# Low parts of the weights of q, k, v, z and gates: a negated copy by ScalarE and an adding transfer in place of VectorE's subtraction

## The chip, the cores and the metric

One core of a Trainium2 chip runs the whole program. The metric is the device time of one execution in microseconds (us). The engines are TensorE (PE; its weight loads are PEld), VectorE (DVE), ScalarE (ACT), GpSimd (POOL) and SyncE (SP); a q behind a name (SPq, ACTq, POOLq) is the engine's own queue, from which it issues DMAs.

## What is computed

One layer of a hybrid backbone in fp32, with 512 latent and 256 context tokens and a model width of 1024. Cut to what matters here:

```
h  = modulate(rms(x,   norm_attn), mod_x[0], mod_x[1])
hc = modulate(rms(ctx, norm_attn), mod_c[0], mod_c[1])
qkv, z, beta, decay, cq, ckv, k_rope, gates = split(h @ w_in)   # and the same of hc
q, k, v = silu(conv5(qkv)); q, k l2-normed                      # 8 heads of 128
o_gdn   = chunked gated delta rule over q, k, v, forwards and backwards
o_mla   = softmax attention of 8 heads with low-rank q and kv
y = sigmoid(g_gdn) * (gdn_out(o_gdn, z) @ w_bg) + sigmoid(g_mla) * (o_mla @ w_bm)
x = x + mod_x[2] * (y @ w_out)
x = x + mod_x[5] * (relu(modulate(rms(x)) @ w_mlp_in)^2 @ w_mlp_out)
```

## The kernel before

Products with weights are made in three matmuls in a rounded fp32 format (fp32r). Both factors are split into a high part, which is the value rounded to that format, and a low part, which is what the rounding took away. `mm3` (lines 183 to 186) adds high by high, high by low and low by high into one PSUM bank.

`wchunk` (lines 165 to 180) brings weights in chunks of 128x512 fp32, 256 KB. For each chunk there are three steps: SyncE issues the load into `wf` (line 177, four buffers), ScalarE writes the high part `wh` (line 178, three buffers), and VectorE, or for some weights GpSimd, writes the low part `wl` (line 179, three buffers). A buffer of `wh` or `wl` is free again when TensorE's last matmul has read it, a buffer of `wf` when the low part has been made:

```
nc.sync.dma_start(wf.rearrange("p (k n) -> p k n", k=step), src[:, k:k + step])
act.copy(wh, wf)
eng.tensor_tensor(wl, wf, f32(wh), ALU.subtract)
```

`project` multiplies 128 output columns, that is two such chunks, with the 512 latent tokens (matmuls of 512 columns) and, for k and v, with the 256 context tokens as well. `gdn_in` does that for the k, v and q of a pair of heads; `convolve` then takes the result from PSUM (lines 466 and 468, ScalarE), applies the five-tap convolution (line 471, four instructions of VectorE) and the silu (lines 473 and 474), and `transposes` (line 487) turns the result. `gdn_gram` builds the decay and the Gram matrices: GpSimd selects the triangles `rh` (line 566), TensorE multiplies them (line 571), ScalarE takes Exp (line 577) and VectorE multiplies (lines 584 and 590). `gdn_prep` inverts a triangular matrix, in 30 steps of VectorE (lines 629 and 630) and several small products. `gdn_chain` runs the recurrence over six blocks in both directions: GpSimd selects `Em` and `Qm` (line 727), TensorE multiplies (lines 751, 766, 786, 802, 805), VectorE makes `rho` (758), the state (794) and the output `ob` (812, 813), ScalarE `y` (773, 778). `power` (line 149) is a power on GpSimd; one of its results is `nk`.

`z_chunk` and `gate_chunk` project the eight groups of 128 columns of z and the sixteen of the gates and store them in DRAM. They have the lowest priority and fill TensorE's time between the parts of the recurrence. In all 48 such groups, 96 chunks, belong to k, v, q, z and gates.

The order of the work is not the code's: a scheduler puts all instructions into a fixed order on each engine, from the code's dependencies, its priorities and estimates of its own. On the chip each engine keeps that order and waits at an instruction until its inputs are there and its output buffer is free. A change of one instruction can therefore move others on every engine.

Of the kernel before, what the change touches and what calls it, by code (L numbers as in the profile page):

```python
# [9 lines left out]
AF = mybir.ActivationFunctionType  # L10
ALU = mybir.AluOpType
# [4 lines left out]
P = 128  # L16
LOW = 1000000
AHEAD = 100
KT = 8
# [59 lines left out]
def f32(ap):  # L79
    return ap.bitcast(F32)  # L80
# [3 lines left out]
def tile_layer(ctx, tc, I, out, stop=None, dbg=None):  # L84
    nc = tc.nc
    act = nc.scalar
    dve = nc.vector
    pool = nc.gpsimd
# [12 lines left out]
    def bank(tag):  # L101
        return ps.tile([P, 512], F32, tag=tag, name=tag, bufs=banks[tag])

    def v4(t):
        return t.rearrange("p (a b) -> p a b", b=128)
# [41 lines left out]
    def power(out_ap, in_ap, n, half):  # L147
        e = expt[:, 1 if half else 0, 0:n]
        pool.tensor_tensor(out_ap, in_ap, e, ALU.pow)
# [12 lines left out]

    WN = 512

    def wchunk(src, nk=KT, n=P, eng=dve, keep=None):

        step = min(nk, WN // n)
        res = []
        for k in range(0, nk, step):
            wf = wp.tile([P, WN], F32, tag="wf", name="wf", bufs=4)[:, :step * n]  # L170
            if keep is None:
                wh = wp.tile([P, WN], F32R, tag="wh", name="wh", bufs=3)[:, :step * n]
                wl = wp.tile([P, WN], F32R, tag="wl", name="wl", bufs=3)[:, :step * n]
            else:
                wh = keep.tile([P, WN], F32R, tag="kh", name="kh", bufs=2 * KEEP)
                wl = keep.tile([P, WN], F32R, tag="kl", name="kl", bufs=2 * KEEP)
            nc.sync.dma_start(wf.rearrange("p (k n) -> p k n", k=step), src[:, k:k + step])
            act.copy(wh, wf)  # L178
            eng.tensor_tensor(wl, wf, f32(wh), ALU.subtract)  # L179
            res += [(wh[:, n * i:n * i + n], wl[:, n * i:n * i + n]) for i in range(step)]  # L180
        return res

    def mm3(po, lh, ll, rh, rl, first, last):
        pe.matmul(po, lh, rh, start=first, stop=False)  # L184
        pe.matmul(po, lh, rl, start=False, stop=False)  # L185
        pe.matmul(po, ll, rh, start=False, stop=last)  # L186
# [148 lines left out]
    for qf in range(4):  # L335
        kts = (qf, qf + 4)
        modulation(qf)
        if qf == 0:
            for k in range(0, KT, 4):
                nc.sync.dma_start(ct[:, k:k + 4, :], I["cxT"][:, k:k + 4, :])  # L340
        for kt in kts:
            modulate(kt, xt, NL, rx, hTh, hTl, 0)
        w = [wchunk(I["w_nat"][:, kt:kt + 1, 384:736], 1, 352) for kt in kts]
        natural(pos1[:4], kts, w)
        if qf == 0:
            rc = rms(ct, NC, 1, "c")
        for kt in kts:
            modulate(kt, ct, NC, rc, cTh, cTl, 1)
        natural(pos1[4:], kts, w)
        if qf == 1:  # L350
            nc.sync.dma_start(mk[:, ncol:], I["masks"][:, ncol:])
            nc.sync.dma_start(mk2, I["early"])
# [57 lines left out]
    for kt in order:  # L410
        natural(pos0, (kt,), [wchunk(I["w_nat"][:, kt:kt + 1, 0:384], 1, 384)])
# [28 lines left out]
    def project(chunk, with_ctx):  # L440
        pl = bank("d")
        pc = bank("d")[:, :NC] if with_ctx else None
        for k0 in (0, 4):
            for kt in range(k0, k0 + 4):
                mm3(pl, *chunk[kt], hTh[:, kt, :], hTl[:, kt, :], kt == 0, kt == KT - 1)
            if with_ctx:
                for kt in range(k0, k0 + 4):
                    mm3(pc, *chunk[kt], cTh[:, kt, :], cTl[:, kt, :], kt == 0, kt == KT - 1)
        return pl, pc
# [12 lines left out]
    def convolve(pl, pc, ch, dst):  # L462

        o = 0 if pc is not None else NC + GAP
        n = NG - o
        act.copy(raw[:, GAP + NC + GAP:GAP + NG], pl)  # L466
        if pc is not None:
            act.copy(raw[:, GAP:GAP + NC], pc)
        act.activation(dst, raw[:, o + 2:o + 2 + n], AF.Identity, scale=convh[:, ch, 2:3])
        for i in (0, 1, 3, 4):  # L470
            dve.scalar_tensor_tensor(dst, raw[:, o + i:o + i + n], convh[:, ch, i:i + 1], dst, ALU.mult, ALU.add)  # L471
        tt = raw[:, o + 2:o + 2 + n]
        act.activation(tt, dst, AF.Tanh)
        dve.scalar_tensor_tensor(dst, tt, 1.0, dst, ALU.add, ALU.mult)
        if pc is not None:
            pool.memset(raw[:, GAP + NC:GAP + NC + GAP], 0.0)

    def transposes(src, nb, tag):

        res = []  # L480
        b = 0
        while b < nb:
            n = min(4, nb - b)
            t = bank(tag)
            for q in range(n):
                c = at(b + q) if nb == 6 else 128 * (b + q)
                pe.transpose(t[:, 128 * q:128 * q + 128], src[:, c:c + 128], ident)  # L487
            res.append((t, b, n))
            b += n
        return res  # L490

    def gdn_in(pr):
        kT = gp.tile([P, 2, NG], F32, tag="kT", name="kT", bufs=2)
        qT = gp.tile([P, 2, NL], F32, tag="qT", name="qT", bufs=2)
        kn = gp.tile([P, 2, 6, P], F32, tag="kn", name="kn", bufs=2)
        vn = gp.tile([P, 2, 6, P], F32, tag="vn", name="vn", bufs=2)
        ssq = gp.tile([P, 2, 6], F32, tag="ssq", name="ssq", bufs=2)
        ssk = gp.tile([P, 2, 6], F32, tag="ssk", name="ssk", bufs=2)
        nk = gp.tile([P, 2, 6], F32, tag="nk", name="nk", bufs=2)
        r2 = gp.tile([P, 2, 6], F32, tag="r2", name="r2", bufs=2)  # L500
        junk = gx.tile([P, P], F32, tag="junk", name="junk")
        for h in range(2):
            hd = 2 * pr + h
            pl, pc = project(wchunk(I["w_qkv"][8 + hd]), True)
            convolve(pl, pc, 8 + hd, kT[:, h, :])
            for t, b, n in transposes(kT[:, h, :], 6, "t"):
                act.copy(kn[:, h, b:b + n, :], v4(t)[:, :n, :])
                for q in range(n):
                    act.activation(junk, kn[:, h, b + q, :], AF.Square, accum_out=ssk[:, h, b + q:b + q + 1])
            dve.tensor_scalar(ssk[:, h, :], ssk[:, h, :], EPS, None, op0=ALU.add)  # L510
            power(nk[:, h, :], ssk[:, h, :], 6, True)
            dve.reciprocal(r2[:, h, :], ssk[:, h, :])
        res = (kT, qT, kn, vn, ssq, ssk, nk, r2)
        gram = gdn_gram(pr, res)
        for h in range(2):
            hd = 2 * pr + h
            vT = gx.tile([P, NG], F32, tag="vT", name="vT")
            pl, pc = project(wchunk(I["w_qkv"][16 + hd]), True)
            convolve(pl, pc, 16 + hd, vT)
            for t, b, n in transposes(vT, 6, "t"):  # L520
                for q in range(n):
                    act.activation(vn[:, h, b + q, :], t[:, 128 * q:128 * q + 128], AF.Copy,
                                   scale=nk[:, h, b + q:b + q + 1])
        for h in range(2):
            hd = 2 * pr + h
            pl, _ = project(wchunk(I["w_qkv"][hd]), False)
            convolve(pl, None, hd, qT[:, h, :])
            for t, b, n in transposes(qT[:, h, :], 4, "t"):
                for q in range(n):
                    act.activation(junk, t[:, 128 * q:128 * q + 128], AF.Square,  # L530
                                   accum_out=ssq[:, h, b + q:b + q + 1])
        return res, gram
# [311 lines left out]
            act.dma_start(d_y[:, hd, :], tz)  # L844

    def gate_chunk(i):
        pz, _ = project(wchunk(I["w_gate"][i]), False)
        tz = gy.tile([P, NL], F32, tag="tanh", name="tg")
        act.activation(tz, pz, AF.Tanh, scale=0.5)
        nc.sync.dma_start(d_gate[i], tz)  # L850

    def z_chunk(hd):
        pz, _ = project(wchunk(I["w_z"][hd]), False)
        tz = gy.tile([P, NL], F32, tag="tanh", name="tz")
        act.activation(tz, pz, AF.Tanh, scale=0.5)
        dve.scalar_tensor_tensor(tz, tz, 1.0, pz, ALU.add, ALU.mult)
        nc.sync.dma_start(d_z[hd], tz)
# [5 lines left out]
    def fill(pr):  # L863
        for kind, i in fills[pr]:
            if kind == "z":
                z_chunk(i)
            else:
                gate_chunk(i)

    ops0, gram0 = gdn_in(0)  # L870
    prep0 = gdn_prep(0, ops0, gram0)
    ops1, gram1 = gdn_in(1)
    with low():
        fill(0)
    gdn_out(0, gdn_chain(0, ops0, prep0))
    prep1 = gdn_prep(1, ops1, gram1)
    ops2, gram2 = gdn_in(2)
    with low():
        fill(1)
# [495 lines left out]
```

## Time and profile before

| what | value |
|---|---|
| median of three runs | 1333.8 us (1332.42 to 1333.87) |
| profiled execution, its own time | 1332.53 us |
| its span in the profile | 1330.7 us |
| mean granted clock of TensorE | 0.984 |
| TensorE busy | 1269.9 us, 95% of the span |
| VectorE busy | 867.2 us, 65% |
| ScalarE busy | 648.2 us, 49% |
| GpSimd busy | 278.5 us, 21% |
| line 179 on VectorE, all weights | 268 instructions, 182.9 us |
| line 178 on ScalarE, all weights | 292 instructions, 177.1 us |

The span is the time from the first to the last instruction in the trace; the execution's own time is 1.8 us longer. Busy time is the time in which an engine worked on instructions. A TensorE that is busy is not always at its peak, because matmuls overlap and their ends are modelled. The granted clock is the share of TensorE's full clock that the chip allowed. A group gives its line, engine, operation and operands, then its busy time and the mean of one in ns, then the idle time of the engine just before and what ended it.

### The profile page before, as it was taken

How to read it: one execution, taken by the hardware profiler on the slowest of the kernel's cores; microseconds unless marked ns; L12 is line 12 of the kernel's file. 1: busy time of each engine (PE TensorE's matmuls, PEld its weight loads, DVE VectorE, ACT ScalarE, POOL GpSimd, SP SyncE). 2: the span in 40 equal slices, each digit the busy share in tenths (PEclk: the TensorE clock that was granted, in tenths of full speed). 3: DMA queues.
4: the chain of work that ended last, by engine and by line, in shares of the span. 5: the costliest groups of instructions: out<-in, count | busy, mean ns of one | idle time of the engine just before them, and what ended most of it. 6: DMA issues, size and time to landing. Idle time of an engine off the chain costs nothing.

```text
span 1330.7 us, 21029 instructions
## 1 busy us (share of the span) xinstructions
PE 1269.9 (95%) x7430; PEld 1112.8 (84%) x7430; DVE 867.2 (65%) x1861; ACT 648.2 (49%) x1666; POOL 278.5 (21%) x372
## 2 busy tenths in 40 slices
PE   5899899998999999989999999999999999999998
PEld 4798787887888888879899998888997888888886
DVE  4656798866688678747778788676885333333332
ACT  4557575336653675356667576323443242242331
POOL 0022423223410431113112221222041010010110
PEclk9999998988999999999999999999999999999999
DMA  9333225210233124441011013766452222222232
GB/s 359 112 110 88 56 71 128 94 41 9 88 103 104 49 76 120 123 143 60 14 46 37 9 40 131 266 209 249 173 177 95 95 95 95 95 96 95 96 112 86
DMA packets 97993, 141.20 MB, mean 106 GB/s; under 512 B 32736, under 2 KB 41952, under 8 KB 97760
## 3 DMA queue, kind: packets, MB, share of 16 engines
q1 hardware_dynamic: 68576, 127.27, 28.8%
q10 hardware_dynamic: 29312, 12.59, 3.8%
q8 instruction: 59, 0.97, 0.3%
q14 instruction: 46, 0.38, 0.1%
HBM read 124.23 MB, written 15.60 MB: 105 GB/s over the span
## 4 chain that ended last, share of the span: by engine, by line
PE 82%; DVE 7%; DMA 4%; ACT 4%; issue 1%; POOL 1%; SPq 0%; DVEq 0%; ACTq 0%; POOLq 0%
PE d L184 20%; PE d L185 20%; PE d L186 20%; DMA wm<-in_w_mod 2%; PE p L184 1%; PE c L766 1%; PE p L185 1%; PE p L186 1%; PE c L786 1%; PE p L1046 1%; PE c L751 1%; PE e L802 1%; DVE kT L471 1%; PE e L805 1%; PE t L487 1%
## 5 line engine op out<-in xcount | busy, mean ns | idle before, releaser
L178 ACT CAST wh<-wf 128x512 fp32r<-128x512 f32 (+2 forms) x292 | 177.1, 610 | 352.2 <-PE d L185 307.4
L179 DVE TENSOR_TENSOR wl<-wf,wh 128x512 fp32r<-128x512 f32 (+2 forms) x268 | 182.9, 686 | 164.2 <-ACT wh L178 161.5
L184 PE MATMUL d<-hTh,wh 128*128 128x512 f32 x384 | 156.2, 407 | 4.2 <-ACT raw L466 3.5
L185 PE MATMUL d<-hTl,wh 128*128 128x512 f32 x384 | 155.0, 404 | 0.0
L186 PE MATMUL d<-hTh,wl 128*128 128x512 f32 x384 | 154.0, 401 | 0.0
L184 PE MATMUL d<-ah,wh 128*128 128x512 f32 x256 | 100.7, 395 | 0.0
L185 PE MATMUL d<-al,wh 128*128 128x512 f32 x256 | 100.7, 395 | 0.0
L186 PE MATMUL d<-ah,wl 128*128 128x512 f32 x256 | 100.6, 395 | 0.0
L1233 POOL TENSOR_TENSOR a<-r 128x512 f32<-128x512 f32 (+1 forms) x36 | 37.1, 1033 | 269.2 <-ACT r L1231 264.8
L184 PEld LDWEIGHTS d<-hTh,wh 128*128 128x128 f32 x384 | 73.7, 192 | 19.8 <-ACT raw L466 5.0
L186 PE MATMUL d<-h2h,wl 128*128 128x512 f32 x224 | 87.4, 390 | 0.9 <-DVE wl L179 0.9
L185 PE MATMUL d<-h2l,wh 128*128 128x512 f32 x224 | 87.2, 389 | 0.0
L184 PE MATMUL d<-h2h,wh 128*128 128x512 f32 x224 | 87.2, 389 | 0.0
L186 PEld LDWEIGHTS d<-hTh,wl 128*128 128x128 f32 x384 | 73.7, 192 | 14.0
L185 PEld LDWEIGHTS d<-hTl,wh 128*128 128x128 f32 x384 | 73.9, 193 | 13.3
L179 POOL TENSOR_TENSOR wl<-wf,wh 128x512 fp32r<-128x512 f32 x24 | 36.2, 1510 | 133.3 <-ACT wh L178 133.3
L1272 DVE SCALAR_TENSOR_TENSOR x<-d,mcol,x 128x512 f32<-128x512 f32 x32 | 24.0, 751 | 61.5 <-PE d L186 61.5
L186 PEld LDWEIGHTS d<-ah,wl 128*128 128x128 f32 x256 | 48.1, 188 | 11.6
L184 PEld LDWEIGHTS d<-ah,wh 128*128 128x128 f32 x256 | 48.1, 188 | 11.5
L185 PEld LDWEIGHTS d<-al,wh 128*128 128x128 f32 x256 | 48.1, 188 | 11.5
L186 PEld LDWEIGHTS d<-h2h,wl 128*128 128x128 f32 x224 | 42.0, 188 | 10.1 <-DVE wl L179 1.4
L184 PEld LDWEIGHTS d<-h2h,wh 128*128 128x128 f32 x224 | 42.0, 188 | 8.7
(552 smaller groups left out, 3468.0 us busy)
## 6 DMA issues: line engine op xcount, KB each, us to landing
wf<-in_w_mi SPq DMA_DIRECT2D x64, 256.0 KB, 2.7
wf<-in_w_mo SPq DMA_DIRECT2D x64, 256.0 KB, 2.6
wf<-in_w_qkv SPq DMA_DIRECT2D x48, 256.0 KB, 2.8
wm<-in_w_mod SPq DMA_DIRECT2D x40, 256.0 KB, 5.4
wm<-in_w_mod SPq DMA_DIRECT2D x16, 512.0 KB, 9.0
wf<-in_w_gate SPq DMA_DIRECT2D x32, 256.0 KB, 2.7
wms<-in_w_mod SPq DMA_DIRECT2D x12, 512.0 KB, 8.5
wf<-in_w_z SPq DMA_DIRECT2D x16, 256.0 KB, 2.7
```

Of the source, the lines that this page charges most:

```text
L178: act.copy(wh, wf)
L179: eng.tensor_tensor(wl, wf, f32(wh), ALU.subtract)
L184: pe.matmul(po, lh, rh, start=first, stop=False)
L185: pe.matmul(po, lh, rl, start=False, stop=False)
L186: pe.matmul(po, ll, rh, start=False, stop=last)
L471: dve.scalar_tensor_tensor(dst, raw[:, o + i:o + i + n], convh[:, ch, i:i + 1], dst, ALU.mult, ALU.add)
L487: pe.transpose(t[:, 128 * q:128 * q + 128], src[:, c:c + 128], ident)
L751: pe.matmul(t[:, 0, h, :], kT[:, h, at(bs[d]):at(bs[d]) + 128], S_[d][:, h, :], start=True, stop=True)
L766: pe.matmul(t[:, 0, h, :], Em[d][:, h, :], rho[d][h], start=True, stop=True)
L786: pe.matmul(t[:, 0, h, :], kn[:, h, bs[d], :], y2[d][:, h, :], start=True, stop=True)
L1233: pool.tensor_tensor(a_, r, r, ALU.mult)
L1272: dve.scalar_tensor_tensor(x1[:, ot, :], po, mcol[:, 5, ot, 0:1], x1[:, ot, :], ALU.mult, ALU.add)
```

## The change

For q, k, v, z and gates the low part is made in another way. ScalarE reads the loaded chunk, negates it and writes it into `wl`; since `wl` is fp32r, what is written is the negated high part. Then GpSimd issues a transfer within SBUF that adds the loaded chunk to what stands in `wl`. All other weights keep the subtraction. `gdn_in`, `z_chunk` and `gate_chunk` pass `sums=True` in their five calls; three of them, which read alike, are left out here:

```
-    def wchunk(src, nk=KT, n=P, eng=dve, keep=None):
+    def wchunk(src, nk=KT, n=P, eng=dve, keep=None, sums=False):
...
             act.copy(wh, wf)
-            eng.tensor_tensor(wl, wf, f32(wh), ALU.subtract)
+            if sums:
+                act.activation(wl, wf, AF.Copy, scale=-1.0)
+                pool.dma_start(f32(wl), wf, accum_op=ALU.add)
+            else:
+                eng.tensor_tensor(wl, wf, f32(wh), ALU.subtract)
...
-            pl, pc = project(wchunk(I["w_qkv"][8 + hd]), True)
+            pl, pc = project(wchunk(I["w_qkv"][8 + hd], sums=True), True)
...
-        pz, _ = project(wchunk(I["w_gate"][i]), False)
+        pz, _ = project(wchunk(I["w_gate"][i], sums=True), False)
```

Lines behind the edit are four higher than before: the high part stays line 178, the negated copy is line 180, the transfer 181, the remaining subtraction 183, the matmuls 188 to 190. In the whole program VectorE has 96 instructions fewer, ScalarE 96 more and GpSimd 96 DMA issues more.

On ScalarE, where the second k head is convolved and the first v head follows, it stood before:

```order
L469 ACTIVATE kT<-raw,convh 128x770
L509 ACTIVATE junk,ssk<-kn 128x128 x4
L507 COPY kn<-t 128x256
L509 ACTIVATE junk,ssk<-kn 128x128 x2
L178 CAST wh<-wf 128x512
L473 ACTIVATE raw<-kT 128x770
L178 CAST wh<-wf 128x512
L466 COPY raw<-d 128x512
L468 COPY raw<-d 128x256
```

and now:

```order
L473 ACTIVATE kT<-raw,convh 128x770
L513 ACTIVATE junk,ssk<-kn 128x128 x4
L511 COPY kn<-t 128x256
L513 ACTIVATE junk,ssk<-kn 128x128 x2
L178 CAST wh<-wf 128x512
L180 ACTIVATE wl<-wf 128x512
L477 ACTIVATE raw<-kT 128x770
L178 CAST wh<-wf 128x512
L180 ACTIVATE wl<-wf 128x512
L470 COPY raw<-d 128x512
L472 COPY raw<-d 128x256
```

A negated copy stands behind each cast, ahead of the silu's tanh (473, now 477) and of the copies from PSUM.

On GpSimd, between the selects of the first gram and the clearing of `off`, it stood before:

```order
L566 AFFINE_SELECT rh<-glo 128x256
L149 TENSOR_TENSOR nk<-ssk,expt 128x6
L476 MEMSET raw 128x2
L536 MEMSET off 128x512 x3
L621 MEMSET off 64x12x64 x2
L149 TENSOR_TENSOR nk<-ssk,expt 128x6
L476 MEMSET raw 128x2
L566 AFFINE_SELECT rh<-ghi 128x256
```

and now:

```order
L181 DMA wl<-wf 128x512
L570 AFFINE_SELECT rh<-glo 128x256
L149 TENSOR_TENSOR nk<-ssk,expt 128x6
L181 DMA wl<-wf 128x512
L480 MEMSET raw 128x2
L181 DMA wl<-wf 128x512
L540 MEMSET off 128x512 x3
L625 MEMSET off 64x12x64 x2
L149 TENSOR_TENSOR nk<-ssk,expt 128x6
L181 DMA wl<-wf 128x512
L480 MEMSET raw 128x2
L181 DMA wl<-wf 128x512
```

Five transfers stand among the selects, the powers and the memsets, two of them right behind a power `nk`.

On TensorE, where two column groups of z follow each other (the number behind a name is the tile's; 2564 and 2565, 2599 and 2600 are high and low parts of two chunks), it stood before:

```order
L186 MATMUL d_2569<-hTh_69,wl_2565 128x512
L487 MATMUL t_2453<-mk_81,qT_1910 128x128 x4
L184 MATMUL d_2569<-hTh_69,wh_2564 128x512
L185 MATMUL d_2569<-hTl_70,wh_2564 128x512
L186 MATMUL d_2569<-hTh_69,wl_2565 128x512
L184 MATMUL d_2569<-hTh_69,wh_2564 128x512
L185 MATMUL d_2569<-hTl_70,wh_2564 128x512
L186 MATMUL d_2569<-hTh_69,wl_2565 128x512
L184 MATMUL d_2610<-hTh_69,wh_2599 128x512
L185 MATMUL d_2610<-hTl_70,wh_2599 128x512
L186 MATMUL d_2610<-hTh_69,wl_2600 128x512
```

and now (the same chunks are 2591 and 2592, 2627 and 2628):

```order
L189 MATMUL d_2597<-hTl_70,wh_2591 128x512
L687 MATMUL p_1856<-D1_1801,Vx_1857 128x32 x4
L687 MATMUL p_1856<-D1_1801,Vx_1863 128x32 x4
L491 MATMUL t_2475<-mk_81,qT_1922 128x128 x4
L190 MATMUL d_2597<-hTh_69,wl_2592 128x512
L188 MATMUL d_2597<-hTh_69,wh_2591 128x512
L189 MATMUL d_2597<-hTl_70,wh_2591 128x512
L190 MATMUL d_2597<-hTh_69,wl_2592 128x512
L188 MATMUL d_2597<-hTh_69,wh_2591 128x512
L189 MATMUL d_2597<-hTl_70,wh_2591 128x512
L190 MATMUL d_2597<-hTh_69,wl_2592 128x512
L188 MATMUL d_2640<-hTh_69,wh_2627 128x512
```

Small products of `gdn_prep` (line 687) now stand inside the chunk, so more of TensorE's work lies between one chunk's matmuls and the next.

## Rows read from the trace of the kernel before

**Rows 1.** Busy us by engine, PE to POOL, 115 to 593 us; clock, DMA:

```profile
115.00:593.00 478.00, 454.80 (x2733) 400.27 (x2732) 364.13 (x797) 264.15 (x711) 137.37 (x224) 0.97 0.29 83
```

**Rows 2.** The same view, the slice from 299.43 us:

```profile
299.43:332.70 33.27, 28.55 (x187) 25.96 (x187) 22.27 (x52) 20.36 (x69) 12.96 (x24) 0.90 0.03 9
```

**Rows 3.** Who TensorE waited for, 115 to 593 us: total us, times, longest:

```profile
PE e L802 <- DVE ob L813: 4.4, 3, 2.8
PE c L766 <- DVE rho L758: 3.6, 3, 1.9
PE d L184 <- ACT raw L466: 3.5, 4, 1.2
PE e L571 <- DVE A L590: 3.3, 2, 1.9
PE t L487 <- DVE kT L474: 2.4, 3, 1.7
...
PE t L487 <- DVE vT L474: 0.3, 2, 0.2
```

**Rows 4.** Timeline, first and last chunk: start us, us, engine, line:

```profile
77.25 0.69 DVE L179 TENSOR_TENSOR wl<-wf,wh 128x512 fp32r<-128x512 f32 x1 [1.63 <-ACT wh L178]
...
82.48 0.39 PE L186 MATMUL d<-hTh,wl 128*128 128x512 f32 x1
...
574.36 0.39 PE L185 MATMUL d<-hTl,wh 128*128 128x512 f32 x1
574.59 0.39 PE L186 MATMUL d<-hTh,wl 128*128 128x512 f32 x1
...
575.20 0.60 ACT L178 CAST wh<-wf 128x512 fp32r<-128x512 f32 x1
...
575.84 0.69 DVE L179 TENSOR_TENSOR wl<-wf,wh 128x512 fp32r<-128x512 f32 x1 [0.65 <-ACT wh L178]
...
584.37 0.39 PE L186 MATMUL d<-hTh,wl 128*128 128x512 f32 x1
```

**Rows 5.** Groups in 115 to 593 us, and ScalarE's wait before casts:

```profile
L179 DVE TENSOR_TENSOR wl<-wf,wh 128x512 fp32r<-128x512 f32 x87 | 61.6, 709 | 25.4 <-ACT wh L178 23.8 <-PE d L186 1.4
...
L178 ACT CAST wh<-wf 128x512 fp32r<-128x512 f32 x87 | 53.7, 619 | 58.2 <-PE d L185 52.9 <-issue 4.3 <-ACT wh L178 0.4
...
ACT wh L178 <- PE d L185: 52.9, 35, 4.0
```

**Rows 6.** ScalarE's DMA issue (timeline); GpSimd's work on 128x512 (groups):

```profile
342.05 0.33 ACTq L844 DMA_DIRECT2D d_y<-sz  x1
...
L179 POOL TENSOR_TENSOR wl<-wf,wh 128x512 fp32r<-128x512 f32 x24 | 36.2, 1510 | 133.3 <-ACT wh L178 133.3
```

**Rows 7.** GpSimd: line 566 (ns min/median/max), its group, the wait before nk:

```profile
L566 POOL TENSOR_SCALAR_AFFINE_SELECT rh<-ghi x42: 398/498/2226, 128.7 to 490.2; 128x256 fp32r<-128x256 f32 x42
...
L566 POOL TENSOR_SCALAR_AFFINE_SELECT rh<-glo 128x256 fp32r<-128x256 f32 x42 | 29.3, 697 | 2.7 <-PE e L571 2.7
...
POOL nk L149 <- DVE ssk L510: 30.1, 6, 6.6
```

**Rows 8.** DMA issues: KB each, median us from issue to landing:

```profile
wf<-in_w_qkv SPq DMA_DIRECT2D x48, 256.0 KB, 2.8
...
d_y<-sz ACTq DMA_DIRECT2D x8, 256.0 KB, 2.0
...
yt<-d_y SPq DMA_DIRECT2D x8, 256.0 KB, 5.9
```

**Rows 9.** DMA queues: packets, MB, share of 16 engines:

```profile
q1 hardware_dynamic: 68576, 127.27, 28.8%
```

**Rows 10.** Timeline, 256-column matmuls and four fp32 ones (eight records):

```profile
341.45 0.28 PE L185 MATMUL d<-cTl,wh 128*128 128x256 f32 x1
341.57 0.28 PE L186 MATMUL d<-cTh,wl 128*128 128x256 f32 x1
341.69 1.16 PE L766 MATMUL c<-vn,Em 128*128 128x128 f32 x8
```

More of the change, by code (lines that the diff above doesn't have):

```diff
@@ L517, in gdn_in @@
             vT = gx.tile([P, NG], F32, tag="vT", name="vT")
-            pl, pc = project(wchunk(I["w_qkv"][16 + hd]), True)
+            pl, pc = project(wchunk(I["w_qkv"][16 + hd], sums=True), True)
             convolve(pl, pc, 16 + hd, vT)
@@ L525, in gdn_in @@
             hd = 2 * pr + h
-            pl, _ = project(wchunk(I["w_qkv"][hd]), False)
+            pl, _ = project(wchunk(I["w_qkv"][hd], sums=True), False)
             convolve(pl, None, hd, qT[:, h, :])
@@ L852, in z_chunk @@
     def z_chunk(hd):
-        pz, _ = project(wchunk(I["w_z"][hd]), False)
+        pz, _ = project(wchunk(I["w_z"][hd], sums=True), False)
         tz = gy.tile([P, NL], F32, tag="tanh", name="tz")
```

## The prediction

> **What bounds the kernel now.** I read the busy time of a stretch first, then who TensorE waits for, then the groups, the DMA issues and single instructions. The change touches 96 weight chunks, those of k, v, q, z and gates, and all but a few are worked through between 115 and 593 us; that stretch is mine. There TensorE is busy 454.8 of 478 us, VectorE 364.1 (76%), ScalarE 264.2 (55%), GpSimd 137.4 (29%), and the granted clock is 0.97 [rows 1]. So all that any relief can give back there is the 23.2 us that TensorE stands idle, and what the clock costs: at 0.97 the engine ran at the lower of its two levels (1.2 against 2.4 GHz) for 6% of 478 us, which loses half of that, 14.3 us. Low clock comes where the engine had idled: the slice from 299.43 us has 28.55 us busy of 33.27 and a clock of 0.90 [rows 2]. I therefore let each idle microsecond carry 14.3/23.2 = 0.62 us of lost clock. Bound: 37.5 us, 2.8% of the span.
>
> Who ends the idling: the waits of TensorE, in 12 rows from 4.4 down to 0.3 us, sum to 23.1 us: 14.3 on VectorE (4.4 + 3.6 + 3.3 + 2.4 + 0.3 + 0.3), 7.0 on ScalarE, 1.8 on GpSimd [rows 3]. None is a wait for low parts of weights; these come early. In the last chunk the buffer's previous user ends at 574.98 (574.59 and 0.39 long), the cast starts at 575.20, the subtraction ends at 576.53, 1.55 us after the release, and the matmul that first reads the low part starts at 584.37, 7.8 us later [rows 4]. The first chunk has 4.5 us so (77.94 to 82.48) [rows 4]. Over all 96 chunks the delay that could be added before TensorE notices has a median of 6.8 us; it is under 5 us for 19 of them and under 3 for five.
>
> **The change, part by part.** The loads on SyncE stay the same; 96 subtractions leave VectorE, ScalarE gets 96 negated copies, GpSimd 96 transfers. The matmuls are the same in number and stand in another order, as the rows ahead show.
>
> *VectorE.* In the stretch 87 of the 96 subtractions, of 709 ns, 61.6 us in all, go [rows 5]: 364.1 becomes 302.5, 76% becomes 63%. What that is worth is only what TensorE waits for VectorE's convolutions, rho, A and ob. Between nothing and all of the 14.3 us I take half, because a queue's waiting goes roughly as load/(1 − load), 3.2 before and 1.7 after. With the clock, 7.15 x 1.62 = **−11.6 us** (bounds 0 and −23.2).
>
> *ScalarE.* 87 negated copies of the cast's shape, at the cast's 619 ns, are 53.9 us [rows 5]: 55% becomes 67%, load/(1 − load) goes from 1.23 to 1.99, so 7.0 us of waits would become 11.3. Behind each negated copy stand the convolution's copies and tanh, the grams' Exp and Bt; TensorE waits for these. But 35 of the 87 casts come after idling for the buffer's release [rows 5], that is when ScalarE had nothing else ready, so I take 60% of the 4.3 us: 2.6 x 1.62 = **+4.2 us** (bounds 0 and +7.0).
>
> *GpSimd.* The trace has no DMA issue on it. ScalarE and SyncE issue theirs in 0.33 us [rows 6]; GpSimd's own work on a 128x512 tile takes 1.51 us [rows 6]. I take 1.0 us, in between, since the nearest rows by form are issues and those by engine are slow. 87 of them make 29% into 47%; load/(1 − load) goes from 0.40 to 0.88, so 1.8 us of waits could become 4.0. TensorE waited only five times for it; I take half of the 2.2 added: 1.1 x 1.62 = **+1.8 us** (bounds 0 and +3.6). Each transfer also waits, in GpSimd's order, for ScalarE's copy, with the selects rh, Em and Qm and the power nk behind it; and it can itself stand behind nk, which waited 30.1 us for VectorE in the stretch [rows 7].
>
> *The transfer.* It reads the loaded tile, reads the negated one and writes the sum, all in SBUF, 256 KB each. The trace has no such transfer. From below, a 256 KB write from SBUF lands 2.0 us after its issue; a load in 2.8 [rows 8]. From above, the slowest 256 KB loads, in a busy queue, take 5.9 us [rows 8]. One 256 KB stream costs 28.8% x 1330.7 us x 0.262/127.27 = 0.79 us of all 16 engines [rows 9]; the second read adds that once. I take 1.0 + 2.8 + 0.8 = 4.6 us from GpSimd's turn to landing (range 2.0 to 1.5 + 5.9 = 7.4), nearest to the loads, which are the same size in the same pieces. After a release the low part is then ready in 1.55 + 4.6, about **6.2 us**, 1.55 now.
>
> The Trainium skill (DMA: Bandwidth & Descriptors, Anatomy of one DMA — SWDGE (gpsimd) path) fits a transfer issued from GpSimd as about 2.0 us plus bytes over 436 GB/s, an estimate of 2.6 us here; no row of this trace has one. By it the low part is ready in some 4.2 us, and the ring's term below is nothing.
>
> *Is that early enough?* The low parts go round three buffers. In the new order I counted, for each chunk, the matmuls between the last one that must be over before the transfer can go (the last reader of its buffer, or a later one for which a GpSimd or ScalarE instruction ahead of it waits) and the first one that reads the chunk. At 0.228 us for 512 columns and 0.12 for 256, which are the distances of neighbouring starts [rows 4, 10], and 0.22 for an fp32 matmul of 128 columns, two records of 0.11 each in the trace (eight took 1.16 with the last one's end) [rows 10], TensorE has 5.7 us of its own work in the worst case and 9.4 in the median. One chunk has less than 6 us, ten less than 7, 29 less than 8, 40 less than 9; the missing time sums to 0.3, 4.5, 25 and 62 us. At 6.2 us the ring costs almost nothing; for chance delays I take **+1.2 us**. Loads: a loaded tile is now held until the transfer lands instead of the subtraction's end, 4.6 us longer; with four of them and the load landing in 2.8 us, it is there two chunks ahead, and I cost that at nothing. If this cover went, ScalarE's cast would wait for SyncE's load. The transfers' 0.8 to 1.6 us of the engines per chunk fit beside a DMA share of 0.29 [rows 1].
>
> *Sum:* −11.6 + 4.2 + 1.8 + 1.2 = **−4.4 us**. The profiled execution took 1332.5 us (span 1330.7 and 1.8 around it); the median of the three runs is 1.3 us higher. That makes 1328.1 there and **1329.4 us** as a median.
>
> **The rivals.** *The transfer is slow* (slower). Place: the ring of three low parts. It decides from about 8 us between release and landing, that is a transfer of 6.4 us, between my 4.6 and the upper end of 7.4. One stall of TensorE also covers the two chunks behind it, so the missing 25 us cost between a third and all of it: +8 to +25 before any lost clock; at 9 us, +20 to +62. With the sum's other terms (−5.6) that is 1336 to 1353 at 8 us. For it: two reads, and GpSimd's selects, 398 ns at best, have a mean near 700 and a maximum of 2226 beside VectorE [rows 7], so its time is not its own. Against it: the stretch's own 256 KB loads and writes land in 2.8 and 2.0 us [rows 8].
> The Trainium skill (SBUF — State Buffer, SBUF: two separate sides) says descriptors of such a transfer are written by GpSimd, which VectorE locks out in its two-port modes, so that a 0.62 us transfer took 3.1: 2.5 us more, about 8.7 us after the release, an estimate inside this rival; no run here shows it yet.
>
> *GpSimd's order* (slower): a transfer that waits for ScalarE holds the selects of the grams and the chain, or nk waiting for VectorE holds a transfer. nk waited up to 6.6 us [rows 7]; three such places of half that, with the clock, are 3 x 3 x 1.62 = +14.6, against −6.2 for the other terms: 1342, and 1337 with two.
>
> *ScalarE takes VectorE's place* (no change): both upper bounds hold, 7.0 us there and 3.6 on GpSimd: −11.6 + 7.0 + 3.6 + 1.2 = +0.2, 1334.
>
> *VectorE's queue was the whole cause*: all of its 14.3 us go, −23.2 + 7.2 = −16.0: 1318.
>
> **How the numbers follow.** About 0.2% (2.7 us) is what a measurement of this kernel can tell from no change. The forecast, 1325 to 1331, has 0.33, since each of its four terms is read from a row but the factor on each is mine; the full relief 0.09; ScalarE in VectorE's place 0.21; the slow transfer 0.25, as its price is the only one without a row; GpSimd's order 0.12. So faster 0.42, same 0.21, slower 0.37. The range from 1318, the full relief, to 1352, near the slow transfer's end at 8 us, leaves out about 0.15, nearly all above. The likeliest case's own range is 1325 to 1331.
>
> **What would show it.** Right: VectorE's line 179 group (183 there now) with 172 instructions; TensorE's waits on VectorE near 7 us in the stretch; transfers landing in 4 to 5 us; no waits of line 190 (the low part's matmul) on a DMA beyond 2 us; a clock of 0.98. Wrong: waits of line 190 of 10 us or more, transfers over 6 us, GpSimd's waits on ScalarE's line 180 with TensorE waiting for rh or Em behind them, or ScalarE's waits above 12 us.

## The result, and the profile after

The changed kernel took 1346.93 us (median of four runs, 1344.08 to 1350.96) beside 1333.11 us for the kernel before (median of four as well): ratio **1.0116, 95% interval 1.0089 to 1.0143**. The prediction said 1329.4, 4.4 us faster; it came out 1.16% slower, some 15 us by the ratio and 13.8 by the medians, inside the range but on the other side. The profiled execution is the slowest of the four, 1350.96 us with a span of 1349.3.

The groups that the change touches, in the whole program of the changed kernel (the lines that answer to [rows 5] and [rows 6]):

```profile
L183 DVE TENSOR_TENSOR wl<-wf,wh 128x512 fp32r<-128x512 f32 (+2 forms) x172 | 114.9, 672 | 127.5 <-ACT wh L178 126.5 <-PE d L189 0.7
...
L180 ACT ACTIVATE wl<-wf 128x512 fp32r<-128x512 f32 x96 | 60.6, 632 | 2.4 <-PE p L189 2.1 <-PE d L190 0.3
...
L181 POOL DMA_DIRECT2D wl<-wf x96 | 85.6, 891 | 173.4 <-ACT wl L180 128.3 <-ACT y L782 9.2 <-ACT junk L513 7.7
```

The change did what it says: 172 subtractions left on VectorE, a negated copy costs 632 ns (619 assumed), an issue on GpSimd 0.89 us (1.0 assumed). GpSimd spent 128.3 us waiting for negated copies, 52 times.

The stretch from 115 to 593 us, answering to [rows 1], with the same columns:

```profile
115.00:593.00 478.00, 448.14 (x2697) 394.39 (x2696) 313.11 (x704) 303.81 (x796) 199.21 (x313) 0.97 0.57 127
```

VectorE fell from 364.1 to 313.1 us and ScalarE rose to 303.8, near the 302.5 and 318 of the prediction. TensorE was busy 448.1 us in place of 454.8, so it stood idle longer, and the clock did not rise. The column that moved most is the last but one: the 16 DMA engines were busy 0.57 of the time, 0.29 before.

Who TensorE waited for in that stretch, answering to [rows 3] (total us, times, longest):

```profile
PE e L806 <- DVE ob L817: 5.1, 4, 2.8
PE c L770 <- DVE rho L762: 4.2, 3, 2.6
PE t L491 <- DVE kT L478: 4.2, 3, 3.5
PE d L188 <- ACT raw L470: 4.0, 4, 1.4
PE e L593 <- ACT QK L581: 2.8, 1, 2.8
PE e L575 <- DVE A L594: 2.7, 2, 1.8
...
PE d L190 <- DMA wl<-wf: 0.2, 1, 0.2
```

The waits on VectorE grew although it has less to do: with the rows left out, 18.9 us where the prediction hoped for 7 and before had 14.3. A low part that came late cost TensorE 0.2 us, once. So the ring of three buffers was never the trouble. The transfers landed well within what the prediction allowed (line 181 on GpSimd: ns min/median/max of the issue, then the landing):

```profile
L181 POOL DMA_DIRECT2D wl<-wf x96: 852/874/1678, 79.2 to 594.4; - x96
...
DMA to landing us min/median/max: 3.3/3.7/6.8
```

What did change is some of the other transfers. DMA issues of the changed kernel, KB each and median us to landing:

```profile
d_gate<-tg SPq DMA_DIRECT2D x16, 256.0 KB, 3.5
...
dB<-pt ACTq DMA_DIRECT2D x8, 192.0 KB, 3.9
D<-dB ACTq DMA_DIRECT2D x8, 192.0 KB, 5.6
```

and of the kernel before, the same three (`pt<-dA`, the end of an earlier round trip, stayed at 3.8 us, and `yt<-d_y` fell from 5.9 to 5.0):

```profile
d_gate<-tg SPq DMA_DIRECT2D x16, 256.0 KB, 2.2
...
dB<-pt ACTq DMA_DIRECT2D x8, 192.0 KB, 3.1
D<-dB ACTq DMA_DIRECT2D x8, 192.0 KB, 3.5
```

`dB` and `D` are a round trip through DRAM by which `gdn_prep` rearranges the inverted blocks; `pt` comes from one ahead of it. What follows in the recurrence needs `D`. Where the time went, by landmarks in the two traces (us from the span's start): the first matmul that reads a low part of the changed weights starts 1.9 us later (82.5 and 84.4), the last matmul with the gates' weights 15.4 us later (588.2 and 603.6), the end of TensorE's work 19.6 us later. Of the 19.6 us, 13.5 arise where k, v, q, z and gates are projected. 3.3 arise in the attention behind it (its first and last transposes start 14.7 and 18.0 us later), whose work is the same and only its order differs.

### The profile page after: what moved, and what is told of

The parts are those of the page before. It is cut to its first block, busy times and chain, and to the rows that moved or that the text cites. A ratio compares the mean times of both kernels' runs of the same rounds, so it can differ in the third digit from the quotient of the medians.

```text
span 1349.3 us, 21273 instructions
## 1 busy us (share of the span) xinstructions
PE 1272.2 (94%) x7430; PEld 1113.3 (83%) x7430; DVE 817.4 (61%) x1765; ACT 695.6 (52%) x1762; POOL 347.8 (26%) x468
## 3 DMA queue, kind: packets, MB, share of 16 engines
q0 software_dynamic: 13824, 25.17, 11.2%
## 4 chain that ended last, share of the span: by engine, by line
PE 67%; DVE 11%; DMA 7%; ACT 6%; issue 3%; POOL 1%; ACTq 0%; SPq 0%; DVEq 0%; POOLq 0%
PE d L188 16%; PE d L190 16%; PE d L189 16%; DMA D<-dB 1%; PE p L1050 1%; DVE tu L633 1%; PE p L188 1%; PE p L189 1%; DMA dB<-pt 1%; DMA pt<-dA 1%; PE p L190 1%; PE c L790 1%; DVE pt L634 1%; ACT wl L180 1%; DVE pp L1040 1%
## 5 line engine op out<-in xcount | busy, mean ns | idle before, releaser
L183 DVE TENSOR_TENSOR wl<-wf,wh 128x512 fp32r<-128x512 f32 (+2 forms) x172 | 114.9, 672 | 127.5 <-ACT wh L178 126.5
L181 POOL DMA_DIRECT2D wl<-wf x96 | 85.6, 891 | 173.4 <-ACT wl L180 128.3
L190 PEld LDWEIGHTS d<-hTh,wl 128*128 128x128 f32 x384 | 74.0, 193 | 14.7 <-DMA wl<-wf 0.6
L180 ACT ACTIVATE wl<-wf 128x512 fp32r<-128x512 f32 x96 | 60.6, 632 | 2.4 <-PE p L189 2.1
```

The source lines that it names most:

```text
L180: act.activation(wl, wf, AF.Copy, scale=-1.0)
L181: pool.dma_start(f32(wl), wf, accum_op=ALU.add)
```

## The experiments

Each kernel is compared with the kernel before on the same chip. Rows of the table stem from different sessions, so a difference between two of them carries both intervals. A change of one instruction sends the scheduler's order another way, so first the ruler:

| kernel | ratio to the kernel before | 95% interval |
|---|---|---|
| before, same work in a second order | 0.9948 | 0.9925 to 0.9972 |
| changed, second order | 1.011 | 1.0069 to 1.015 |
| relief alone, two orders | 0.992; 0.9946 | 0.9892 to 0.9948; 0.9925 to 0.9967 |
| copy alone, two orders | 1.0055; 1.0045 | 1.0037 to 1.0074; 1.0028 to 1.0063 |
| relief and copy, no transfer | 0.9996 | 0.9974 to 1.0017 |
| transfer alone, two orders | 1.014; 1.0194 | 1.011 to 1.017; 1.0165 to 1.0222 |
| issues of one column alone | 1.0017 | 0.999 to 1.0044 |
| changed, adding one column, two orders | 1.0064; 1.0036 | 1.0039 to 1.0089; 1.0018 to 1.0055 |
| changed, plain copy of one column | 1.0021 | 0.9999 to 1.0042 |
| changed, plain whole copy by GpSimd | 1.0038 | 1.0016 to 1.006 |
| changed, plain whole copy by SyncE | 1.0035 | 1.0007 to 1.0064 |
| change for z and gates only | 1.0013 | 0.9995 to 1.0032 |
| change for k, v, q only | 1.0049 | 1.0027 to 1.007 |
| z and gates subtracted on GpSimd | 1.0202 | 1.0165 to 1.0238 |

**The order.** The cast is spelled as a copy scaled by 1.0, in the kernel before and in the changed one:

```
-            act.copy(wh, wf)
+            act.activation(wh, wf, AF.Copy, scale=1.0)
```

> The kernel before, with the cast spelled as a copy scaled by 1.0: the same work on every engine, but the scheduler puts 1325 of TensorE's lines elsewhere. Theory D (the order alone costs it): off the kernel before by 0.4% or more in either direction. Otherwise a ratio within 0.3% of 1. This is also the measure of what a difference between two kernels of this case is worth.

> The changed kernel with the same spelling of the cast: the same work, 423 of TensorE's lines elsewhere. If its order alone made the loss, the ratio moves by 0.4% or more off 1.0116; if the added work makes it, it stays within 0.3% of that.

The kernel before gained 0.52% (1323.97 against 1329.08 us), though each cast became 10 ns longer; the changed one stayed at 1.011. So the loss is not one unlucky order (mean of two orders against mean of two, it is 1.4%), and a single ratio within half a per cent of another says little. The respelled kernel before is also the fastest of all that leave no part of the computation out or changed.

**The copy alone.** ScalarE's negated copy is written, and VectorE's subtraction overwrites it:

```
             act.copy(wh, wf)
+            if sums:
+                act.activation(wl, wf, AF.Copy, scale=-1.0)
             eng.tensor_tensor(wl, wf, f32(wh), ALU.subtract)
```

> VectorE keeps its 96 subtractions; ScalarE writes the negated copy into wl besides, and the subtraction overwrites it. So ScalarE's 54 us are added in the stretch and nothing else. Theory A (ScalarE's queue holds the convolutions and grams): most of the loss is here, 1340 to 1348 us. Theory B (the transfers load the 16 DMA engines, and the chain's round trips through DRAM take longer): 1333 to 1336, and D<-dB lands in 3.5 us as before. Theory C (GpSimd's queue waits for ScalarE and holds selects): 1333 to 1336. Theory D (the scheduler's other order alone costs it): 1340 or more, with stalls in the attention too. The prediction's own term was +4.2, 1337.

> The copy alone (subtractions kept) with the cast spelled as a copy scaled by 1.0: the same work in another order, as a second sample, since order alone was worth -0.52% on the kernel before. If the copy's +0.55% is the copy's: 1.003 to 1.008. If it was the order's: 0.995 to 1.002.

Measured +7.3 and +7.2 us against the runs beside them. The copy costs something, about half of the whole loss, and more than the +4.2 that was forecast; against the mean of the two orders of the kernel before it is about 10 us.

**The relief alone.**

```
             if sums:
-                act.activation(wl, wf, AF.Copy, scale=-1.0)
-                pool.dma_start(f32(wl), wf, accum_op=ALU.add)
+                wl = wh
```

> The low parts of these weights are left out: the high part stands in their place in the third matmul (other products than the reference's), so no subtraction, no copy, no transfer. This is the relief of VectorE with nothing paid for it; waiting for the low part goes too. The prediction's term says 1333 - 11.6 = 1321.5, with TensorE's waits on VectorE in the stretch halved from 14.3 to about 7 us. Rival: the relief is worth little, because those waits are the latency of chains and not VectorE's load: 1330 to 1334, waits on VectorE still 12 us or more. Theory D: anything, 1340 included.

> The relief alone (the high part stands in for the low one, nothing else) in a second order, 1724 of TensorE's lines elsewhere. If the -0.8% is the relief's: 0.987 to 0.997, and below the second order of the kernel before (0.9948) by as much as 0.8% if orders and relief add. If it was the order's: 0.995 to 1.002.

Measured -9.5 and -6.6 us. In the first of them TensorE still waited for VectorE, in 115 to 593 us:

```profile
PE e L805 <- DVE ob L816: 4.4, 3, 2.8
PE t L490 <- DVE qT L477: 3.2, 1, 3.2
PE c L769 <- DVE sz L846: 2.5, 1, 2.5
PE t L490 <- DVE vT L477: 2.2, 1, 2.2
PE t L490 <- DVE kT L477: 1.8, 1, 1.8
```

With the three smaller rows that is 16.6 us, and 12.3 in the second order, where [rows 3] have 14.3. So these waits did not halve when VectorE's load fell (364.1 to 315.3 us busy in the stretch); that they are the length of chains fits, but no run here singles it out. Nor is the gain less idling: from the first to the last 512-column matmul with the weights of the change, TensorE idled 21.6 us with the relief and 20.7 before. It ran 17.1 us at the lower clock there and 27.3 before, which is 5 of the 7 us by which this stage is shorter. The second order missed its forecast: it was to be faster than the second order of the kernel before by as much as 0.8% if orders and relief add, and 0.9946 against 0.9948 is no difference. So the relief's own size lies anywhere from nothing to 0.8%, 0.4% as mean of two orders against mean of two.

**Relief and copy without the transfer.** The low part stays the negated high part.

```
                 act.activation(wl, wf, AF.Copy, scale=-1.0)
-                pool.dma_start(f32(wl), wf, accum_op=ALU.add)
```

> The changed kernel without the transfer (the low part is then the negated high part, other products than the reference's): relief and copy alone, in one kernel. From the runs of each, -0.67% + 0.50%: ratio 0.994 to 1.002. If relief and copy do not add like that, that is if ScalarE's queue takes the place of VectorE's: 1.003 to 1.008. What the small transfer (1.0064) has above this is GpSimd's issue and wait; what the changed kernel (1.0116) has above the small transfer is bytes.

0.9996: VectorE's gain and ScalarE's loss cancel. The whole loss of 1.16% comes with the transfer.

**The transfer alone.** VectorE subtracts, and the transfer then adds into the same tile:

```
             act.copy(wh, wf)
+            eng.tensor_tensor(wl, wf, f32(wh), ALU.subtract)
             if sums:
-                act.activation(wl, wf, AF.Copy, scale=-1.0)
                 pool.dma_start(f32(wl), wf, accum_op=ALU.add)
-            else:
-                eng.tensor_tensor(wl, wf, f32(wh), ALU.subtract)
```

> VectorE keeps its subtractions and the adding transfer goes behind each; there is no negated copy (the low parts then hold the weight as well, so the products are not the reference's). Transfers, DMA share 0.57 and GpSimd's issues as in the changed kernel; GpSimd waits for VectorE in place of ScalarE. Theory A: 1333 to 1336. Theory B: 1343 to 1350, D<-dB at 5 us or more. Theory C: 1338 to 1345, with POOL waiting 60 us or more for low parts. Theory D: 1340 or more. The prediction's terms were +1.8 and +1.2, 1336.

> The transfer alone (subtractions kept, no negated copy; low parts hold the weights as well) in a second order, 1688 of TensorE's lines elsewhere. If the +1.4% is the transfer's: 1.009 to 1.019. If half of it was the order's: 1.003 to 1.009.

+19.4 us (1348.91 against 1329.48) and +27.8, the second just above its forecast. It overstates the transfer in the changed kernel: here GpSimd waits for VectorE's subtraction, and TensorE and its weight loads do wait for low parts:

```profile
PEld d L188 <- DMA wl<-wf: 8.2, 11, 2.2
...
PE d L188 <- DMA wl<-wf: 4.8, 8, 2.0
```

**GpSimd's issues.** Three kernels with hardly a byte. To the kernel before is added, per chunk, a transfer of one column that nobody reads:

```
+                pool.dma_start(spare[:, turn[0]:turn[0] + 1], wf[:, 0:1], accum_op=ALU.add)
```

> The kernel before, and for each of the 96 chunks GpSimd issues besides an adding transfer of one column of the loaded tile into a spare column that nobody reads. GpSimd's 85 us of issues without bytes, without the negated copy, without a wait for ScalarE, and nobody waits for the transfer. From the runs so far, the small transfer left a loss of 0.64% where relief and copy alone give -0.8 + 0.55, so issues with their waits would be worth +0.89%. Theory E (it is the issue's 0.9 us in GpSimd's order, ahead of selects): ratio 1.005 to 1.010. Theory C (it is GpSimd waiting for ScalarE's copy): 0.998 to 1.003, and the waits do not show.

And the changed kernel with one column in place of 512, adding, then plain, and with the adding one in another order (the negated copy ahead of the cast):

```
-                act.activation(wl, wf, AF.Copy, scale=-1.0)
-                pool.dma_start(f32(wl), wf, accum_op=ALU.add)
+                act.activation(wl, wf, AF.Copy, scale=-1.0 / 1024)
+                pool.dma_start(f32(wl)[:, 0:1], wf[:, 0:1], accum_op=ALU.add)
```

> The changed kernel with transfers of one column in place of 512 (same 96 issues on GpSimd, same waits, hardly any bytes; low parts are then wrong but for one column, the negated copy is scaled by 1/1024). Theory A: as the changed kernel, 1344 to 1350. Theory B: the loss goes, 1325 to 1336, D<-dB lands in 3.5 us. Theory C: as the changed kernel, 1342 to 1350, POOL waits for wl near 110 us. Theory D: as the changed kernel if the order stays the same.

> The small transfer (one column) as a plain copy in place of an adding one, in the same order on TensorE and GpSimd. Only GpSimd's issue gets shorter, 0.56 for 0.89 us if it is as with whole tiles, 32 us in all. If GpSimd's issue time is what the adding costs: the ratio falls from 1.0064 to 1.003 or less. If it is the load on the DMA engines: it stays within 0.25% of 1.0064.

> The small adding transfer with ScalarE's negated copy written ahead of its cast: the same work, nearly all of TensorE's lines in another order. If 1.0064 is what the issues and GpSimd's waits for ScalarE cost: 1.004 to 1.009. If it was half the order's, as the pairs so far differ by up to 0.5%: 0.999 to 1.003.

85 us of issues without a wait for ScalarE came to +0.17%, which the runs can't tell from nothing. The small adding transfer, 1338.28 us, fell between the forecasts of the theories B and C, so neither the bytes nor GpSimd's waits alone explain the loss. In the changed kernel the small adding transfers stand at 1.0064 and 1.0036, the small plain ones, in the order of the first on every engine, at 1.0021. GpSimd's line in these two, adding and plain:

```profile
L181 POOL DMA_DIRECT2D wl<-wf x96 | 85.5, 891 | 159.6 <-ACT wl L180 134.4 <-ACT kn L511 5.3 <-ACT nres L276 4.9
```

```profile
L181 POOL DMA_DIRECT2D wl<-wf x96 | 53.2, 554 | 170.7 <-ACT wl L180 145.7 <-ACT kn L511 5.7 <-ACT nres L276 5.2
```

The issue of an adding transfer is 0.34 us longer, whatever its size. By the forecast for this pair, the fall to 1.0021 (1.003 or less) speaks for the issue's time. But their intervals touch, the second order's 1.0036 lies between its two forecasts, and in the two traces that share an order 2.6 us of difference are there before the first chunk: only 1.4 us more arise in the stage, and 2.4 are left at the end. Above the 0.9996 without any transfer, issues and waits on GpSimd cost 0.25 to 0.68%, and whether the longer issue has a part in that stays open.

**Adding against plain copying.** The closest pair. The transfer is the changed kernel's but does not add:

```
-                pool.dma_start(f32(wl), wf, accum_op=ALU.add)
+                pool.dma_start(f32(wl), wf)
```

> The changed kernel with GpSimd's transfer as a plain copy in place of an adding one (the low parts are then the weights, other products than the reference's). TensorE's order is that of the changed kernel, line for line, and so are the waits. SyncE's plain copies took 0.66 us of the 16 engines each, the adding ones 1.5. Theory B (bytes and time on the DMA engines): the ratio falls from 1.0116 to 1.005 to 1.008, D<-dB from 5.6 to near 4 us. Theory C or E (GpSimd's order and waits): it stays at 1.010 to 1.013.

1.0038 in place of 1.0116 (1.011 in the second order), in the same order on every engine, with the same loads and nearly the same waits of GpSimd for ScalarE (135.3 against 128.3 us). It lies below what was forecast for either theory, with `D<-dB` above the 4 us that went with theory B. GpSimd's waits are thereby not what makes the difference; its issue, which is shorter here too, is not ruled out. The stretch with the plain copy:

```profile
115.00:593.00 478.00, 453.68 (x2756) 400.43 (x2754) 313.63 (x713) 307.70 (x800) 170.11 (x313) 0.98 0.42 131
```

GpSimd's group:

```profile
L181 POOL DMA_DIRECT2D wl<-wf x96 | 53.7, 559 | 173.0 <-ACT wl L180 135.3 <-ACT junk L513 8.2 <-ACT y L782 7.6
```

and the DMA issues, KB each and median us to landing:

```profile
wl<-wf POOLq DMA_DIRECT2D x96, 256.0 KB, 2.6
...
dB<-pt ACTq DMA_DIRECT2D x8, 192.0 KB, 3.1
D<-dB ACTq DMA_DIRECT2D x8, 192.0 KB, 4.9
```

The bytes are nearly the same (131 and 127 GB/s), the DMA share is 0.42 and not 0.57. The queue of GpSimd's transfers, with the plain copy and then in the changed kernel (packets, MB, share of 16 engines):

```profile
q0 software_dynamic: 7680, 25.17, 5.0%
```

```profile
q0 software_dynamic: 13824, 25.17, 11.2%
```

Over 96 transfers that is 5.0% x 1334.2 / 96 = 0.69 us of all 16 engines for a plain one and 11.2% x 1349.3 / 96 = 1.57 us for an adding one. Since the order is the same, all 7430 matmul records of the two traces pair up one by one. The changed kernel is 3.5 us behind at the first chunk, 13.7 us at the last matmul with the gates' weights and 15.1 us at the end of the program: 10.3 us are lost in the stage. There TensorE idled 30.5 us in place of 24.5 and spent 30.7 us in place of 23.9 at the lower clock, which costs 3.4. The largest single step, 2.2 us, is a matmul that waits for `rho`. The chain of waits that leads to it, with the plain copy (start us, us, what):

```profile
412.11 0.31 ACTq L639
...
412.44 3.15 DMA dB<-pt
...
415.62 5.44 DMA D<-dB
...
421.08 0.59 DVE T L654
...
421.69 0.56 DVE T L656
422.25 0.52 DVE rho L762 x2
```

and in the changed kernel:

```profile
421.27 0.31 ACTq L639
...
421.60 4.39 DMA dB<-pt
...
426.02 6.09 DMA D<-dB
...
432.13 0.59 DVE T L654
...
432.74 0.56 DVE T L656
433.30 0.53 DVE rho L762 x2
...
433.97 0.68 PE c L770 x4
```

From issue to `rho` it is 10.14 us and 12.03 us; both round trips took longer, by 1.24 and 0.65. VectorE stands idle meanwhile and `rho` stands behind `D` in its order. Its waits on the round trips, 80 to 610 us, in the changed kernel and then with the plain copy (the kernel before had 8.4 and 5.1):

```profile
DVE D L655 <- DMA D<-dB: 16.0, 4, 6.7
...
DVE tu L633 <- DMA pt<-dA: 9.3, 4, 3.7
```

```profile
DVE D L655 <- DMA D<-dB: 8.6, 3, 4.5
...
DVE tu L633 <- DMA pt<-dA: 5.4, 3, 3.0
```

The difference of the two, 7.4 + 3.9 = 11.3 us, is of the size of the 10.3 us that TensorE lost, but this doesn't show that the one makes the other. Such waits come without any whole transfer too, as in the kernel with relief and copy alone (0.9996), same window:

```profile
DVE D L654 <- DMA D<-dB: 12.8, 4, 6.1
...
DVE tu L632 <- DMA pt<-dA: 6.1, 3, 2.6
```

They sum to 18.9 us there, and to 25.9 in the last kernel below, which has no transfer within SBUF at all; VectorE's waits do not follow the loss. The transfers themselves speak for the slower round trip. All 24 of `pt`, `dB` and `D` together take 105.7 us from issue to landing in the changed kernel and 104.7 in its second order, where `D` is just as slow:

```profile
D<-dB ACTq DMA_DIRECT2D x8, 192.0 KB, 5.7
```

In every other kernel of this document they take 77 to 91 us (84.2 before, 90.5 with the plain copy). Against it stands the transfer alone: as many adding transfers at a DMA share of 0.56, and 90 us. Followed back from the last matmul with the gates' weights, from each wait to what ended it, the changed kernel's path runs through transfers to and from DRAM (the round trips, and those of z and y) that took 10.8 us longer than with the plain copy, and GpSimd's instructions add 1.6. The path of the kernel with the plain copy runs through fewer transfers, which took 2.6 us less than in the changed one. So slower transfers may account for anything from 2.6 to all of the 10.3 us. That adding in place of copying costs 0.78% in the same order (0.4 to 1.1) is measured; that it does so through the round trips is an inference.

**SyncE in GpSimd's place.**

```
-                pool.dma_start(f32(wl), wf, accum_op=ALU.add)
+                nc.sync.dma_start(f32(wl), wf)
```

> The changed kernel with the transfer issued by SyncE as a plain copy of the loaded tile over the negated one (the low parts are then the weights themselves, other products than the reference's). Two streams of 256 KB in place of three, nothing on GpSimd; SyncE waits for ScalarE's copy in place of GpSimd, and its loads stand behind. Theory C or E (GpSimd's order): the loss of the transfer goes but for a part of the bytes, ratio 0.998 to 1.004. Theory B (bytes on the DMA engines): 1.006 to 1.012, with D<-dB at 5 us. If SyncE's loads suffer, ScalarE's cast waits for DMA wf 20 us or more, and the time says nothing on GpSimd.

1.0035, inside the forecast for theories C and E, and `D<-dB` at 4.0 us, not 5. But GpSimd's own plain copies came to the same 1.0038, though in another order. So GpSimd's waits for ScalarE, 135.3 us there and none here, cost nothing that shows above the half per cent that an order is worth.

**The place.** The change for half of the chunks:

```
-        pz, _ = project(wchunk(I["w_gate"][i], sums=True), False)
+        pz, _ = project(wchunk(I["w_gate"][i]), False)
...
-            pl, pc = project(wchunk(I["w_qkv"][8 + hd], sums=True), True)
+            pl, pc = project(wchunk(I["w_qkv"][8 + hd]), True)
```

> The change for z and gates alone (48 of the 96 chunks, those that fill TensorE between the parts of the recurrence); k, v, q keep VectorE's subtraction. If the loss is from transfers that run beside the recurrence's own round trips through DRAM: most of it is here, 1.008 to 1.014. If it is from copies and transfers ahead of the convolutions of k, v and q: 0.996 to 1.003. If it goes by the number of chunks: 1.004 to 1.007.

> The change for k, v and q alone, 48 of the 96 chunks; z and gates keep VectorE's subtraction. z and gates alone gave 1.0013. If the rest of the loss sits at k, v, q: 1.008 to 1.013. If the two halves only hurt together (load on the DMA engines that has slack up to some level): 0.998 to 1.005.

The lower pair of lines, and its like for v and q, is the first kernel; the upper, and its like for z, the second. 0.13% and 0.49% add up to 0.62%, half of the whole change's 1.16%. DMA shares in the stretch were 0.46 and 0.41. Neither place is to blame alone; the loss grows faster than the number of transfers, though with the order worth half a per cent that is a hint.

**Another way to relieve VectorE.**

```
-        pz, _ = project(wchunk(I["w_gate"][i]), False)
+        pz, _ = project(wchunk(I["w_gate"][i], eng=pool), False)
```

and the same for z.

> The kernel before with the 48 subtractions of z and gates on GpSimd in place of VectorE (1.5 us each, 72 us more on GpSimd): half of the relief with no transfer and no copy. If half of the relief holds (-0.33%) and GpSimd's extra time is worth as little as that of the issues alone (+0.17%): 0.994 to 1.001. If its long instructions hold the selects: 1.003 to 1.010.

1.0202, beyond both forecasts and worse than the change. GpSimd's busy time in the stretch (188.09 us) is less than with the transfers, but one subtraction takes it 1.43 us. TensorE's waits sum to 19.4 us on VectorE (14.3 before) and 4.4 on GpSimd (1.8), so selects held up by long instructions are only a part; where the rest comes from was not tested. GpSimd's group and the first rows of TensorE's waits (115 to 605 us):

```profile
L179 POOL TENSOR_TENSOR wl<-wf,wh 128x512 fp32r<-128x512 f32 x72 | 103.0, 1431 | 221.4 <-ACT wh L178 187.3 <-DMA yt<-d_gate 26.9 <-issue 4.5
```

```profile
PE e L802 <- DVE ob L813: 5.9, 4, 2.8
PE c L786 <- ACT y L773: 4.2, 2, 3.7
PE e L571 <- POOL rh L566: 3.9, 3, 2.6
```

## Why the prediction was wrong

*The step that failed* is the one that put the transfers' load on the DMA engines at nothing, the sentence that ends "fit beside a DMA share of 0.29". The load itself was priced rightly, 0.8 to 1.6 us of the engines per chunk, and is 1.57. What was missing is its cost: with transfers 1.0116, without 0.9996: 1.2%, about 16 us, where the two terms for GpSimd and the ring had 3.0. Of it 0.78% is the adding and some 0.4% what a plain copy costs as well. The prediction looked for late low parts, and for what held loads back, and never asked which other transfers stand on the path that ends the stage: the share doubled to 0.57, and `D<-dB` went from 3.5 to 5.6 us. How much of the 1.2% comes by that way, and how much by the longer issue of adding transfers, stays open.

*VectorE, -11.6.* Measured -9.5 and -6.6 against the order of before, and less, about -5.5, against the mean of its two orders. Size inside the bounds, reason wrong: TensorE's waits on VectorE did not halve; they were 16.6 and 12.3 us with the relief alone.

*ScalarE, +4.2.* Mis-sized: +7.3 and +7.2, just beyond the upper bound of +7.0, and about +10 against the mean of the two orders of before. Relief and copy together came to nothing, where the sum had -7.4. That is about a third of the miss.

*GpSimd, +1.8.* The issue took 0.89 us, near the 1.0 assumed. By itself it measured +0.17% (-0.1 to +0.44), which fits. That GpSimd's order became a bound is not shown: with SyncE in its place a plain copy cost the same. With the waits for ScalarE the issues cost 0.25 to 0.68%, 3 to 9 us, which is more than the term and leaves this rival a part.

*The ring, +1.2, and the landing.* Right: 3.7 us from issue to landing where 4.6 was assumed with the issue in it, and 0.2 us of waiting by TensorE. The slow transfer as the prediction had it, by way of the ring, falls. The Trainium skill (DMA: Bandwidth & Descriptors, Anatomy of one DMA — SWDGE (gpsimd) path) gave an estimate of 2.6 us. The plain copies landed in just that, the adding ones in 3.7. The Trainium skill (SBUF — State Buffer, SBUF: two separate sides) has a transfer of 0.62 us take 3.1 while VectorE locks GpSimd out, from which the prediction made 2.5 us more. Here the issue's median is 0.874 us and its longest 1.678, so no such delay shows in the issue; 12 of the 96 landings took over 5 us, and no run tells what held those up.

*The rivals.* The time, 1346.9, lies inside the slow transfer's 1336 to 1353, which is luck, since the ring cost only 0.2 us, and 5 us above GpSimd's order (1337 to 1342), which can have made a part of the loss. The rival that was missing is a slower round trip. Its price could have been bounded from the trace of before: 24 round-trip transfers (`pt`, `dB`, `D`), 84 us from issue to landing in all, on DMA engines whose share doubles.

*The signs that were named.* 172 instructions in line 183's group: seen. Landings of 4 to 5 us: 3.7. No waits for low parts: seen. Waits on VectorE near 7 us and a clock of 0.98: not seen, 18.9 us and 0.97. Of the signs of being wrong none came: 0.2 us of waits for low parts, a median landing of 3.7 us, 1.1 us of waits for `rh`, 9.5 us on ScalarE. They all belonged to rivals that were thought of.

## What to carry to other kernels

Before moving work from an engine onto the DMA engines, list the small transfers that a dependent chain waits for, and price them at the new share: a queue that nobody waits for can still cost time, and here the slowest of the round trips went from 3.5 to 5.6 us beside it. A saving on an engine that is not the bottleneck is worth what a run with that work simply left out gives, and the waits on it can stay as they were. Where a scheduler sets the order, run the same work in a second order first; here that alone moved the time by half a per cent, as much as most of the parts under test.

## What was not expected of the hardware

An adding transfer of 256 KB within SBUF takes 1.57 us of the 16 DMA engines, a plain copy of the same tile 0.69, at the same bytes counted and 144 against 80 packets each. It lands 3.7 us after its issue, the plain one in 2.6; with one column 2.2 and 1.9 us. Its issue holds GpSimd 0.89 us against 0.56, with one column as with 512 (0.89 and 0.55).
